# Score matmuls on 128 stacked rows, projections due units ahead, and weight splits moved to ScalarE and GpSimd

## The chip, the cores and the metric

The kernel runs on one core of one Trainium2 chip. The metric is device time in microseconds (us); the time before is 1441.4 us, the median of three runs (1441.32 to 1442.19). Names used below: TensorE is PE, VectorE is DVE, ScalarE is ACT, GpSimd is POOL, SyncE is SP (it issues the DMAs).

## The reference

One layer of a streaming encoder, on 1024 tokens of width 1024, with 16 heads of 64.

```
h = modulate(rms_norm(x), shift, scale);  q,k,v = split(h @ w_in)      # 8 heads A, 8 heads B
A: scores = q k^T / 8 + relative bias, over the own chunk of 64 and the 8 before; softmax; @ v
B: z = q k^T / 8, strictly causal; weights = sigmoid(z_j) * prod_{later keys} sigmoid(-z); @ v
x = x + gate * (concat(rms_norm(A)*g_a, rms_norm(B)*g_b) @ w_out)
h = modulate(rms_norm(x), ...);  g,u = split(causal depthwise conv(h @ w_up))
x = x + gate * ((silu(g) * u) @ w_down);  out = rms_norm(x) * final_g
```

Everything is float32. The kernel works in split numbers: an operand is kept as a high part rounded to the matmul format and a low part, the difference; a product is high x high + high x low + low x high.

## The kernel before, in words

Three stages follow each other. The first loads x, computes the modulation and the norm, transposes h into `hT` (features on partitions) and projects q and k of the first pair of heads. The second is attention, and the only stage whose matmuls the diff changes. The third is the rest of the output projection and the feed-forward part.

In the attention stage there are 8 pairs of heads; pairs 0 to 3 are stick-breaking (B), 4 to 7 chunked (A). Each pair has 16 units: 4 groups `g` of 256 queries, 2 heads `h`, 2 blocks `u` of 128 queries. The loop over `i` (L902) emits for every step the scores of unit i+2, the transposes of unit i's weights (L767) and, after a second block, their product with v (`pv`, L788). Weights of a B unit: sigmoid of z and of -z on ACT, a product scan on DVE (L762), a multiplication on POOL (L765). Weights of an A unit: bias and maximum on DVE, exp on ACT, scaling on POOL (L758).

Between these pieces `fill` (L632) emits matmuls of a list of jobs in a fixed order: projections of q and k (`job_qk`, 48 matmuls of 512 columns for one of them) and of v (`job_v`, 24 matmuls of 256 columns for each block of tokens), then the output projection. A job may not begin before unit `e` and is due at unit `d`; `quota` (L651) spreads the planner's costs (216 and 109 ns a matmul) evenly between these. The order of PE's instructions is the order in which the code emits them; other engines' instructions are placed by a scheduler, in order on each engine's queue. In the background `mods` (L893) accumulates the later modulation on DVE (`macc`, L875) from weights that SP loads one piece ahead.

A weight tile (512 KB) is loaded when a job begins or the one before does (`prefetch`), rounded by DVE (`split_w`, L122) and its low part taken in four pieces (L125), on DVE for q, k and v.

A projected half of 512 tokens lies in PSUM with both heads of the pair on its 128 rows. For the scores a query tile holds q's high part on the 64 rows of the head and its low part on the other 64; the key tile `kh` holds the high part twice. One matmul of 128 rows gives both products with the high keys; a second, of 64 rows, adds high queries x low keys (`kl`):

```
pe(te.matmul, s[:, 0:w], lt, pr.kh[h][:, c], start=True, stop=False)
pe(te.matmul, s[:, 0:w], lt[a], pr.kl[a, c], start=False, stop=True)
```

`evac_q` and `evac_k` (L151, L163) make the high part on ACT and the low part on DVE, and SP's DMAs copy them to the rows where they are wanted: four for a half of q, four for a half of k. The first pair is written in place (L174, L182). There are six query tiles, of which a pair uses four.

Of the kernel before, what the change touches and what calls it, by code (L numbers as in the profile page):

```python
# [12 lines left out]
F32R = mybir.dt.float32r  # L13
# [6 lines left out]
P = 128  # L20
# [6 lines left out]
NP = 8  # L27
# [28 lines left out]
def build(nc, tc, t, ctx):  # L56
# [61 lines left out]
    def split_w(raw, shape, eng=ve):  # L118
# [3 lines left out]
        ve.tensor_copy(wh, raw)  # L122
# [25 lines left out]
    def ex_tile():  # L148
        return mk(pq, [P, HALF + 12], F32R, "ex")[:, 0:HALF]

    def evac_q(ps, hf, qs):  # L151

        x, y = (ex_tile() for _ in range(2))
        sc.activation(x, ps, AF.Copy, scale=HD ** -0.5)
        ve.scalar_tensor_tensor(y, ps, HD ** -0.5, f(x), ALU.mult, ALU.subtract)
        for h in range(2):
            a, b = (lo64, hi64) if h == 0 else (hi64, lo64)
            d = mk(pq, [P, HALF], F32R, "qs")
            sy.dma_start(f(d[a]), f(x[a]))
            sy.dma_start(f(d[b]), f(y[a]))  # L160
            qs[h][hf] = d

    def evac_k(ps, hf, kh, kl):  # L163

        cols = slice(hf * HALF, (hf + 1) * HALF)
        x = ex_tile()
        sc.copy(x, ps)
        ve.tensor_sub(kl[:, cols], ps, f(x))
        for h in range(2):
            a = lo64 if h == 0 else hi64  # L170
            for b in (lo64, hi64):
                sy.dma_start(f(kh[h][b, cols]), f(x[a]))

    def evac_q0(ps, hf, qs):  # L174
        for h in range(2):
            a, b = (lo64, hi64) if h == 0 else (hi64, lo64)
            d = mk(pq, [P, HALF], F32R, "qs")
            sc.activation(d[a], ps[a], AF.Copy, scale=HD ** -0.5)
            ve.scalar_tensor_tensor(d[b], ps[a], HD ** -0.5, f(d[a]), ALU.mult, ALU.subtract)
            qs[h][hf] = d  # L180

    def evac_k0(ps, hf, kh, kl):  # L182
        cols = slice(hf * HALF, (hf + 1) * HALF)
        for h in range(2):
            a, b = (lo64, hi64) if h == 0 else (hi64, lo64)
            sc.copy(kh[h][a, cols], ps[a])
            ve.tensor_sub(kl[a, cols], ps[a], f(kh[h][a, cols]))
            sy.dma_start(f(kh[h][b, cols]), f(kh[h][a, cols]))
# [12 lines left out]
    def new_k(pr):  # L201
        pr.kh = [mk(pq, [P, S], F32R, "kh") for _ in range(2)]
        pr.kl = mk(pq, [P, S], F32R, "kl")
# [243 lines left out]
    for hf in range(2):  # L447
        evac_q0(acc0[0][hf], hf, pairs[0].qs)
        evac_k0(acc0[1][hf], hf, pairs[0].kh, pairs[0].kl)
# [18 lines left out]
    def job_qk(p, which, hfs, w):  # L468
# [3 lines left out]
        for hf in hfs:  # L472
            ps = mk(ps1, [P, HALF], F32, "mm")
            yield from mm3g(ps, [((w[0][0][:, kb], w[0][1][:, kb]), hT[kb][hf]) for kb in range(KB)], 216)
            if which == 0:
                evac_q(ps, hf, pr.qs)
            else:
                evac_k(ps, hf, pr.kh, pr.kl)
# [119 lines left out]
    def add_qk(p):  # L598
        for which in (1, 0):
            add(lambda which=which: pre_qk(p, which), lambda w, which=which: job_qk(p, which, (0, 1), w),  # L600
                48 * 216, 16 * (p - 2) + 14 if which else 16 * (p - 1) + 4, 16 * p - 3)

    def add_v(g):
        got = []

        def pre():
# [4 lines left out]
        for tb in range(TB):  # L611
# [3 lines left out]
    add_v(0)  # L615
    add_qk(1)
    for g in range(1, 4):
        add_qk(2 * g)
        add_v(g)
# [859 lines left out]
```

## Time and profile before

| | |
|---|---|
| median of three runs | 1441.4 us |
| the profiled execution, its own time | 1439.25 us |
| its span (first to last instruction) | 1437.5 us |
| busy: PE, DVE, ACT, POOL | 1362.3, 1231.0, 596.7, 792.9 us |
| attention stage | from about 75 to 648 us |
| granted PE clock over the span | 0.986 |

Busy time is the union of an engine's instructions. Matmuls are pipelined and the end of each is modelled, so PE counts as busy also where one matmul follows the other late; how fast it really goes is read from the distance between starts. An instruction's mean contains the time that it waits inside the engine. "Idle before" is the time in which the engine stood still ahead of an instruction, with what ended it. A tile's name is the program's (`S` scores, `mm` projections, `T` transposes and the product with v, `kt` and `pb` the factors of the weights, `raw`, `wh`, `wl` a weight as loaded, its high and its low part).

### The profile page before, as it was taken

How to read it: one execution, taken by the hardware profiler on the slowest of the kernel's cores; microseconds unless marked ns; L12 is line 12 of the kernel's file. 1: busy time of each engine (PE TensorE's matmuls, PEld its weight loads, DVE VectorE, ACT ScalarE, POOL GpSimd, SP SyncE). 2: the span in 40 equal slices, each digit the busy share in tenths (PEclk: the TensorE clock that was granted, in tenths of full speed). 3: DMA queues.
4: the chain of work that ended last, by engine and by line, in shares of the span. 5: the costliest groups of instructions: out<-in, count | busy, mean ns of one | idle time of the engine just before them, and what ended most of it. 6: DMA issues, size and time to landing. Idle time of an engine off the chain costs nothing.

```text
span 1437.5 us, 19602 instructions
## 1 busy us (share of the span) xinstructions
PE 1362.3 (95%) x6580; PEld 1077.5 (75%) x6580; DVE 1231.0 (86%) x2135; ACT 596.7 (42%) x1246; POOL 792.9 (55%) x678
## 2 busy tenths in 40 slices
PE   5899999999999999999887999999999999999996
PEld 3786788678877887777675777777777777777774
DVE  7879999988878767776789889899998899998888
ACT  5545554555454444342433233333333333233334
POOL 4624343434422225664568666677667677667664
PEclk9999999999999999999989999999999999999998
DMA  8533533343245237646110111111111211111213
GB/s 310 177 118 91 144 89 87 94 123 95 74 126 162 79 112 210 216 155 249 44 45 15 54 50 60 51 45 45 59 52 47 63 45 44 53 56 45 67 37 117
DMA packets 75246, 136.69 MB, mean 95 GB/s; under 512 B 9081, under 2 KB 35849, under 8 KB 75146
## 3 DMA queue, kind: packets, MB, share of 16 engines
q1 hardware_dynamic: 75146, 135.44, 30.6%
q8 instruction: 52, 0.85, 0.2%
q14 instruction: 48, 0.39, 0.1%
HBM read 102.89 MB, written 18.88 MB: 85 GB/s over the span
## 4 chain that ended last, share of the span: by engine, by line
PE 42%; DVE 39%; ACT 6%; issue 5%; DMA 4%; POOL 3%; SPq 0%; DVEq 0%; POOLq 0%; ACTq 0%
PE mm L140 15%; PE up L1086 12%; DVE y L1095 9%; PE T L140 5%; PE dnf L140 5%; PE S L140 4%; DVE x L1220 4%; ACT y L1091 3%; DVE y L1028 3%; DVE ah L1029 2%; DVE kt L762 2%; DVE macc L875 2%; DMA rawm<-ada 2%; DVE ptl L785 1%; DVE wl L125 1%
## 5 line engine op out<-in xcount | busy, mean ns | idle before, releaser
L1220 DVE TENSOR_TENSOR x<-dnf,x 128x512 f32<-128x512 f32 x340 | 222.4, 679 | 0.1
L1095 DVE SCALAR_TENSOR_TENSOR y<-y,sm,y 128x512 f32<-128x512 f32 (+2 forms) x160 | 191.8, 1199 | 28.5 <-ACT y L1091 28.4
L1086 PE MATMUL up<-h,wh 128*128 128x512 f32 x640 | 199.6, 393 | 2.0 <-ACT y L1128 1.2
L1052 POOL TENSOR_TENSOR wl<-raw,wh 128x1024 fp32r<-128x1024 f32 (+1 forms) x62 | 160.1, 2584 | 63.0 <-ACT wh L1050 56.4
L765 POOL TENSOR_TENSOR pb<-pb,kt 128x512 f32<-128x512 f32 (+2 forms) x96 | 91.6, 967 | 158.9 <-DVE kt L762 126.2
L1091 ACT ACTIVATE y<-y,sm 128x512 f32<-128x512 f32 x80 | 65.4, 817 | 262.6 <-DVE y L1167 134.7
L140 PE MATMUL mm<-H,wh 128*128 128x512 f32 x448 | 158.2, 419 | 0.0
L140 PE MATMUL dnf<-dh,ah 128*128 128x512 f32 x336 | 133.6, 397 | 10.5 <-DVE x L1220 9.3
L1086 PEld LDWEIGHTS up<-h,wh 128*128 128x128 f32 x640 | 119.1, 189 | 31.2 <-ACT y L1128 4.2
L140 PE MATMUL dnf<-dl,ah 128*128 128x512 f32 x336 | 134.4, 400 | 2.2 <-POOL dl L1198 0.5
L140 PE MATMUL dnf<-dh,al 128*128 128x512 f32 x336 | 132.7, 395 | 0.9 <-DVE al L1030 0.9
L1086 PE MATMUL up<-h,wl 128*128 128x512 f32 x320 | 125.4, 392 | 0.0
L758 POOL TENSOR_SCALAR pb<-pb,ri 128x640 f32<-128x640 f32 (+2 forms) x64 | 45.6, 713 | 136.0 <-DVE ri L757 84.8
L784 ACT CAST pth<-T 128x512 fp32r<-128x512 f32 (+2 forms) x192 | 86.8, 455 | 65.9 <-PE T L140 64.7
L785 DVE TENSOR_TENSOR ptl<-T,pth 128x512 fp32r<-128x512 f32 (+2 forms) x192 | 98.4, 514 | 10.4 <-ACT pth L784 9.3
L140 PE MATMUL mm<-wh,H 128*128 128x256 f32 x512 | 106.6, 294 | 0.1
L1086 PE MATMUL up<-Tc,wh 128*128 128x512 f32 x320 | 101.0, 397 | 4.6 <-ACT y L1112 4.5
L1198 POOL TENSOR_TENSOR dl<-modt,dh 128x512 fp32r<-128x512 f32 x42 | 65.3, 1554 | 67.9 <-ACT dh L1197 67.9
L1195 POOL TENSOR_TENSOR modt<-modt,modt 128x512 f32<-128x512 f32 x44 | 68.7, 1561 | 58.6 <-DMA modt<-w_down 54.8
L140 PEld LDWEIGHTS mm<-H,wh 128*128 128x128 f32 x448 | 80.1, 189 | 24.0 <-issue 10.8
L140 PE MATMUL T<-ident,pb 128*128 128x128 f32 x528 | 90.4, 275 | 5.8 <-DVE o L810 3.7
L140 PE MATMUL mm<-H,wl 128*128 128x512 f32 x224 | 93.2, 416 | 0.0
(211 smaller groups left out, 3455.5 us busy)
## 6 DMA issues: line engine op xcount, KB each, us to landing
raw<-w_up SPq DMA_DIRECT2D x44, 512.0 KB, 3.6
rawm<-ada SPq DMA_DIRECT2D x128, 128.0 KB, 2.2
modt<-w_down SPq DMA_DIRECT2D x44, 256.0 KB, 2.7
adaw<-ada SPq DMA_DIRECT2D x16, 512.0 KB, 6.6
raw<-w_qk SPq DMA_DIRECT2D x16, 512.0 KB, 3.7
kh<-ex SPq DMA_DIRECT2D x56, 128.0 KB, 2.7
qs<-ex SPq DMA_DIRECT2D x56, 128.0 KB, 2.3
tbd<-wh SPq DMA_DIRECT2D x18, 256.0 KB, 2.3
```

The source lines that it names most:

```text
L140: r = fn(*a, **k)
L758: gp.tensor_scalar(pt[:, 0:n], pt[:, 0:n], ri, 0.0, ALU.mult, ALU.add)
L765: gp.tensor_mul(pt[:, a:b], pt[:, a:b], kt[:, a + 1:b + 1])
L784: sc.copy(dh, tp[:, 0:b - a])
L785: ve.tensor_sub(dl, tp[:, 0:b - a], f(dh))
L1052: late.append(lambda a=a, z=z: ko(gp.tensor_sub(wl[:, a:z], raw[:, a:z], f(wh[:, a:z]))))
L1086: ko(te.matmul(ps, w[x][:, kb], b[kb][y], start=start and n == 0, stop=n == 11, skip_group_check=True))
L1091: ko(sc.activation(y[:, a:z], src[:, a:z], AF.Identity, scale=cw[2][:, b], bias=cb[:, b]))
L1095: ko(ve.scalar_tensor_tensor(y[:, o:z], src[:, o - d:z - d], cw[2 - d][:, b], y[:, o:z], ALU.mult, ALU.add))
L1195: ko(gp.tensor_mul(raw, raw, gbc[hf]))
L1198: ko(gp.tensor_sub(wl, raw, f(wh)))
L1220: r = ve.tensor_add(xc, ps, xc)
```

## The change

Both score matmuls have 128 rows. The key tile holds the high part on the head's rows and the low part on the other 64. There are two query tiles for a half and head: one has high and low parts as the keys have them, the other has them exchanged; the two matmuls add up all four products (low x low is new). `kl` goes. A half of q takes eight DMAs, a half of k four as before; in the first pair the second query tile is made by DMAs and the keys need none. Eight query tiles make one pair, so one set serves all pairs in turn; a half of q is a job of its own, and its evacuation waits until the loop has passed the units that still read the old half. For the last pair the second half goes into a spare value tile. Keys and the first half of q are due five units ahead of the pair; the second half of q three units into it; the jobs of v go half before and half after q. A job without matmuls left is finished at once. Weights of q, k and v, and the first two of the feed-forward stage, are rounded on ACT, and low parts are taken on POOL (one of the first two value weights keeps DVE for its low part).

```diff
-    "qs": 6, "kh": 4, "kl": 2, "ex": 2, "vs": 3, "nm": 3, "rs": 4, "ri": 4,
+    "qs": 8, "kh": 4, "ex": 2, "vs": 3, "nm": 4, "rs": 4, "ri": 4,
...
-    def split_w(raw, shape, eng=ve):
+    def split_w(raw, shape, eng=gp):
...
-        ve.tensor_copy(wh, raw)
+        sc.copy(wh, raw)
...
+    def evac_q(ps, hf, qs, tile_of):
+        x, y = (mk(pq, [P, HALF + 12], F32R, "ex")[:, 0:HALF] for _ in range(2))
         sc.activation(x, ps, AF.Copy, scale=HD ** -0.5)
         ve.scalar_tensor_tensor(y, ps, HD ** -0.5, f(x), ALU.mult, ALU.subtract)
         for h in range(2):
-            a, b = (lo64, hi64) if h == 0 else (hi64, lo64)
-            d = mk(pq, [P, HALF], F32R, "qs")
+            a, b = halves(h)
+            d, e = tile_of(), tile_of()
             sy.dma_start(f(d[a]), f(x[a]))
             sy.dma_start(f(d[b]), f(y[a]))
-            qs[h][hf] = d
+            sy.dma_start(f(e[a]), f(y[a]))
+            sy.dma_start(f(e[b]), f(x[a]))
+            qs[h][hf] = d, e
...
+    def evac_k(ps, hf, kh):
         cols = slice(hf * HALF, (hf + 1) * HALF)
-        x = ex_tile()
+        x, y = (mk(pq, [P, HALF + 12], F32R, "ex")[:, 0:HALF] for _ in range(2))
         sc.copy(x, ps)
-        ve.tensor_sub(kl[:, cols], ps, f(x))
+        ve.tensor_sub(y, ps, f(x))
         for h in range(2):
-            a = lo64 if h == 0 else hi64
-            for b in (lo64, hi64):
-                sy.dma_start(f(kh[h][b, cols]), f(x[a]))
+            a, b = halves(h)
+            sy.dma_start(f(kh[h][a, cols]), f(x[a]))
+            sy.dma_start(f(kh[h][b, cols]), f(y[a]))
...
+            sy.dma_start(f(e[b]), f(d[a]))
+            sy.dma_start(f(e[a]), f(d[b]))
+            qs[h][hf] = d, e
...
-            ve.tensor_sub(kl[a, cols], ps[a], f(kh[h][a, cols]))
-            sy.dma_start(f(kh[h][b, cols]), f(kh[h][a, cols]))
+            ve.tensor_sub(kh[h][b, cols], ps[a], f(kh[h][a, cols]))
...
-            if which == 0:
-                evac_q(ps, hf, pr.qs)
+            if which:
+                evac_k(ps, hf, pr.kh)
+            elif p == NP - 1 and hf == 1:
+                spare = mk(p1, [P, TB, 4, HD], F32R, "vs").rearrange("p (n c) a b -> p n (c a b)", n=4)
+                spare = iter([spare[:, n] for n in range(4)])
+                evac_q(ps, hf, pr.qs, lambda: next(spare))
             else:
-                evac_k(ps, hf, pr.kh, pr.kl)
+                while now[0] < 16 * p - (2 if hf else 10):
+                    yield None
+                evac_q(ps, hf, pr.qs, q_tile)
...
-            add(lambda which=which: pre_qk(p, which), lambda w, which=which: job_qk(p, which, (0, 1), w),
-                48 * 216, 16 * (p - 2) + 14 if which else 16 * (p - 1) + 4, 16 * p - 3)
+        add(lambda: pre_qk(p, 1), lambda w: job_qk(p, 1, (0, 1), w), 48 * 216, 16 * p - 18, 16 * p - 5)
...
+        add(pre, lambda w: job_qk(p, 0, (0,), w), 24 * 216, 16 * p - 10, 16 * p - 5)
+        add(pre, lambda w: job_qk(p, 0, (1,), w), 24 * 216, 16 * p - (10 if last else 4), 16 * p - 3 if last else 16 * p + 3)
...
     for g in range(1, 4):
-        add_qk(2 * g)
-        add_v(g)
-        add_qk(2 * g + 1)
+        got = []
+        add_k(2 * g)
+        add_v(g, range(4), got)
+        add_q(2 * g)
+        add_v(g, range(4, TB), got)
+        add_k(2 * g + 1)
+        add_q(2 * g + 1)
...
-        while ns > 0 and jobs_at[0] < len(jobs):
+        now[0] = i
+        while jobs_at[0] < len(jobs):
             jb = jobs[jobs_at[0]]
+            if ns <= 0 and (jb.it is None or jb.cost > 0):
+                return
...
-            c = next(jb.it, None)
+            c = next(jb.it, 0)
             if c is None:
+                return
+            if c == 0:
                 jobs_at[0] += 1
...
-            lt = pr.qs[h][qb // 4][:, (qb % 4) * P:(qb % 4 + 1) * P]
-            a = lo64 if h == 0 else hi64
-            pe(te.matmul, s[:, 0:w], lt, pr.kh[h][:, c], start=True, stop=False)
-            pe(te.matmul, s[:, 0:w], lt[a], pr.kl[a, c], start=False, stop=True)
+            lt = [x[:, (qb % 4) * P:(qb % 4 + 1) * P] for x in pr.qs[h][qb // 4]]
+            for x in range(2):
+                pe(te.matmul, s[:, 0:w], lt[x], pr.kh[h][:, c], start=x == 0, stop=x == 1)
```

## Rows read from the trace of the kernel before

**Rows 1.** The page, busy time by engine: us, share of span, instructions.

```profile
PE 1362.3 (95%) x6580; PEld 1077.5 (75%) x6580; DVE 1231.0 (86%) x2135; ACT 596.7 (42%) x1246; POOL 792.9 (55%) x678
```

**Rows 2.** Stretches: length; busy PE, PEld, DVE, ACT, POOL; clock, DMA share, GB/s.

```profile
75.00:365.00 290.00, 282.05 (x1597) 222.61 (x1597) 268.78 (x469) 153.71 (x378) 118.51 (x184) 0.99 0.37 104
365.00:648.00 283.00, 279.52 (x1535) 221.94 (x1533) 213.81 (x694) 125.93 (x375) 111.02 (x136) 1.00 0.48 142
```

**Rows 3.** Chain of waits, 75 to 365 us, shares by line.

```profile
by line: PE mm L140 18.0%; DVE kt L762 10.3%; issue 9.7%; DVE macc L875 9.4%; DMA rawm<-ada 9.3%; DVE ptl L785 6.4%; PE T L140 6.3%; DVE wl L125 5.2%; PE S L140 5.0%; DVE wh L122 2.8%; DVE otl L818 2.6%; DVE S L746 2.4%; DVE o L810 2.0%; AC
```

**Rows 4.** PE in order of time, 84 to 92 us: start, length, instruction, operands.

```profile
84.07 0.28 PE L140 MATMUL S<-kh,qs 128*128 128x256 f32 x1
84.28 0.38 PE L140 MATMUL S<-kl,qs 64*128 64x256 f32 x1
84.59 0.39 PE L140 MATMUL mm<-wh,H 128*128 128x256 f32 x1
...
88.03 0.39 PE L140 MATMUL mm<-wh,H 128*128 128x256 f32 x2
...
88.38 0.40 PE L140 MATMUL mm<-wh,H 128*128 128x256 f32 x2
...
90.45 0.44 PE L140 MATMUL S<-kh,qs 128*128 128x512 f32 x1
...
91.24 0.39 PE L140 MATMUL mm<-wh,H 128*128 128x256 f32 x1
```

**Rows 5.** Instructions of tile S: second score matmul, min/median/max ns, shapes.

```profile
L140 PE MATMUL S<-kl,qs x192: 322/439/502, 76.1 to 642.6; 64*128 64x384 f32 x64, 64*128 64x256 f32 x48, 64*128 64x512 f32 x32, 64*128 64x128 f32 x16
```

**Rows 6.** Groups by line, DVE, 75 to 365 us: busy us, mean ns, idle before.

```profile
L125 DVE TENSOR_TENSOR wl<-raw,wh 128x256 fp32r<-128x256 f32 x52 | 26.1, 534 | 0.1
L122 DVE CAST wh<-raw 128x1024 fp32r<-128x1024 f32 x13 | 14.4, 1110 | 0.0
```

**Rows 7.** The same stretch table for L122 (DVE) and L125 (DVE, POOL) alone.

```profile
365.00:648.00 283.00, 5.05 (x7) 1.00 0.48 142
...
365.00:648.00 283.00, 11.15 (x28) 0.00 (x0) 1.00 0.48 142
```

**Rows 8.** Instructions of tiles wh and wl: rounding on ACT, pieces on POOL.

```profile
L1050 ACT CAST wh<-raw x60: 1030/1051/1058, 759.0 to 1386.1; 128x1024 fp32r<-128x1024 f32 x60
...
L125 POOL TENSOR_TENSOR wl<-raw,wh x12: 719/733/1897, 60.6 to 685.6; 128x256 fp32r<-128x256 f32 x12
```

**Rows 9.** POOL and DVE in order of time, 206 to 212 us.

```profile
206.11 2.32 POOL L765 TENSOR_TENSOR pb<-pb,kt 128x512 f32<-128x512 f32 x2 [3.93 <-DVE kt L762]
...
206.26 2.46 DVE L875 SCALAR_TENSOR_TENSOR macc<-rawm,cact,macc 128x256 f32<-128x256 f32 x2
...
211.75 0.47 DVE L875 SCALAR_TENSOR_TENSOR macc<-rawm,cact,macc 128x256 f32<-128x256 f32 x1
```

**Rows 10.** POOL and PE in order of time: one unit of 1024 keys.

```profile
217.78 2.26 POOL L765 TENSOR_TENSOR pb<-pb,kt 128x512 f32<-128x512 f32 x2 [2.23 <-DVE kt L762]
...
221.45 0.60 PE L140 MATMUL T<-ident,pb 128*128 128x128 f32 x4
```

**Rows 11.** Instructions of tile qs: DMA issues on SP's queue, min/median/max ns.

```profile
L160 SPq DMA_DIRECT2D qs<-ex x28: 461/587/602, 130.6 to 560.1; - x28
```

**Rows 12.** DVE and ACT in order of time, 46 to 50 us.

```profile
46.29 1.76 DVE L122 CAST wh<-raw 128x1024 fp32r<-128x1024 f32 x1
...
49.31 0.78 ACT L291 ACTIVATE H<-t,sh_mix,sc_mix 128x512 fp32r<-128x512 f32 x1 [3.28 <-DVE sc_mix L249]
```

**Rows 13.** POOL in order of time, the start of the feed-forward stage.

```profile
678.70 7.66 POOL L125 TENSOR_TENSOR wl<-raw,wh 128x256 fp32r<-128x256 f32 x8 [2.26 <-DVE wh L122]
```

**Rows 14.** Waits, 75 to 365 us: who for whom, total us, times, longest.

```profile
PE T L140 <- DVE ptl L785: 4.1, 6, 1.6
...
DVE macc L875 <- DMA rawm<-ada: 3.9, 5, 1.5
...
PE T L140 <- DVE o L810: 3.7, 5, 1.6
```

More of the change, by code (lines that the diff above doesn't have):

```diff
@@ L146, in build, with halves @@
     lo64, hi64 = slice(0, HD), slice(HD, P)
[L148 to L153, printed above, removed]
+    def halves(h):
+        return (lo64, hi64) if h == 0 else (hi64, lo64)
+    def evac_q(ps, hf, qs, tile_of):
+        x, y = (mk(pq, [P, HALF + 12], F32R, "ex")[:, 0:HALF] for _ in range(2))
         sc.activation(x, ps, AF.Copy, scale=HD ** -0.5)
@@ L202, in new_k @@
         pr.kh = [mk(pq, [P, S], F32R, "kh") for _ in range(2)]
-        pr.kl = mk(pq, [P, S], F32R, "kl")
     cps0, ps0 = pool("ps0", space=PSUM)
@@ L448, in build @@
         evac_q0(acc0[0][hf], hf, pairs[0].qs)
-        evac_k0(acc0[1][hf], hf, pairs[0].kh, pairs[0].kl)
+        evac_k0(acc0[1][hf], hf, pairs[0].kh)
     close(cs)
@@ L596, in add, with add_k, add_q, pre @@
         jobs.append(Job(pre, gen, cost, e, d))
-    def add_qk(p):
-        for which in (1, 0):
-            add(lambda which=which: pre_qk(p, which), lambda w, which=which: job_qk(p, which, (0, 1), w),
-                48 * 216, 16 * (p - 2) + 14 if which else 16 * (p - 1) + 4, 16 * p - 3)
-    def add_v(g):
-        got = []
+    def add_k(p):
+        add(lambda: pre_qk(p, 1), lambda w: job_qk(p, 1, (0, 1), w), 48 * 216, 16 * p - 18, 16 * p - 5)
+    def add_q(p):
+        got = []
+        def pre():
+            if not got:
+                got.append(pre_qk(p, 0))
+            return got[0]
+        last = p == NP - 1
+        add(pre, lambda w: job_qk(p, 0, (0,), w), 24 * 216, 16 * p - 10, 16 * p - 5)
+        add(pre, lambda w: job_qk(p, 0, (1,), w), 24 * 216, 16 * p - (10 if last else 4), 16 * p - 3 if last else 16 * p + 3)
+    def add_v(g, tbs, got):
         def pre():
@@ L609, in pre @@
             return got[0]
-        for tb in range(TB):
+        for tb in tbs:
             add(pre, lambda w, tb=tb: job_v(g, tb, w), 24 * 109, 16 * (2 * g - 1) + 2,
                 32 * g + max(0, 4 * (tb // 2) - 2))
-    add_v(0)
-    add_qk(1)
+    add_v(0, range(TB), [])
+    add_k(1)
+    add_q(1)
     for g in range(1, 4):
-        add_qk(2 * g)
-        add_v(g)
-        add_qk(2 * g + 1)
+        got = []
[5 more added lines that the diff above has]
+        add_q(2 * g + 1)
     add(lambda: None, job_out_b, 192 * 216, 0, 126)
@@ L630, in prefetch @@
                     x.w = jobs[j].w
+    now = [0]
     def fill(i, ns):
-        while ns > 0 and jobs_at[0] < len(jobs):
+        now[0] = i
+        while jobs_at[0] < len(jobs):
             jb = jobs[jobs_at[0]]
+            if ns <= 0 and (jb.it is None or jb.cost > 0):
+                return
             if jb.e > i:
```

12 lines of the change are left out of this document (6 added, 6 removed).

## The prediction

> **What bounds the kernel now.** Four views, from wide to narrow. The page gives TensorE (PE) 95% of the span [rows 1], so I first ask whether PE is also full in the stage that the diff touches. The table by stretches [rows 2] splits the attention stage at the change from stick-breaking pairs (75 to 365 us, 64 units) to chunked pairs (365 to 648 us, 64 units): PE is busy 282.05 of 290 and 279.52 of 283 us at a granted clock of 0.99 and 1.00, VectorE (DVE) 268.78 of 290 in the first half and 213.81 of 283 in the second, ScalarE (ACT) about half, GpSimd (POOL) 40%. So PE sets the pace in both halves, and DVE stands close behind it in the first. The chain of waits [rows 3] says the same of the first half: it hops between PE and DVE (scans, products, weight splits), with no long wait in one place. The stalls of PE that another engine causes are short in sum: the two largest of the first half are 4.1 and 3.7 us [rows 14].
>
> Busy is not the same as well used, so the last view is PE in order of time [rows 4], read by the distance from one start to the next. Projections of 256 columns go at 0.35 us for three (88.03 to 88.38), 0.118 us each. The score pair of 256 columns takes 84.07 to 84.59, 0.52 us, where two such matmuls would take 0.24: 0.28 us lost. The pair of 512 columns takes 90.45 to 91.24, 0.79 us against 4 x 0.118 = 0.47: 0.32 lost. The difference lies round the second matmul, the one on 64 rows: 84.07 to 84.28 is 0.21 (0.09 over) and 84.28 to 84.59 is 0.31 (0.19 over). Every change from 128 to 64 rows and back costs time in which PE counts as busy.
>
> **The change part by part.** All is summed on the profiled execution: span 1437.5 us, its own time 1439.25; the median of the runs shown is 1441.4, 2.15 higher, which I add at the end.
>
> *Stacked scores.* There are 192 pairs, of which 32 have 512 columns [rows 5]. Both matmuls now have 128 rows and as many columns as before, so 160 x 0.28 + 32 x 0.32 = 55 us leave PE. Bounds: 192 x 0.28 = 54 if the wide ones lose no more than the others, 192 x 0.32 = 61 if all lose as much as the widest; below, 192 x 0.19 = 36 if only the return from 64 rows is saved. The trace has no score pair with both on 128 rows; I take 55, because the projections, which change weights at every matmul and accumulate into one tile too, run without a gap.
>
> *Weights.* In the attention stage 52 + 28 low pieces and 13 + 7 roundings leave DVE: 26.1 + 14.4 = 40.5 us in the first half [rows 6], 11.15 + 5.05 = 16.2 in the second [rows 7]. ACT gets 20 roundings of 1.05 us (the same shape, which ACT rounds in the feed-forward stage) = 21 us, POOL 80 pieces of 0.73 = 58.6 us, 38 us of it in the first half [rows 8]. PE does not wait for these, since weights are fetched a job ahead; DVE in the first half falls to 228 us. ACT (153.71 + 14) and POOL (118.51 + 38) stay well under the new span. On ACT a rounding waits for its load as it did on DVE; queued behind it are the sigmoids and the high parts of the transposed weights, for which the unit's scan and PE wait: 0, since a load lands long before its job, at most 20 x 1.05 = 21. What POOL costs DVE is below.
>
> *Does DVE follow?* PE's first half shrinks by 96 pairs, 28 us, to about 262 us. DVE with 228 us is under that, at 87%, if POOL does not slow it. It will a little: two macc updates that lie beside POOL's products take 2.46 us together, one alone takes 0.47 [rows 9], so an overlap can cost up to 0.73 us more, once per piece. Lower bound 0; upper bound 52 x 0.73 = 38 us of DVE, none of it beside anything else. The scan and macc, which read and write SBUF alone, are 19.7 of DVE's 41 points in the chain [rows 3], about half; half of the pieces meeting one of them, for half a piece each, is a quarter of the bound, 10 us, and that I take: DVE 238 of 262, 91%, against 93% now. The stalls should then stay what they are; I add 2 us for units that are shorter by a tenth while the chain scan, product, transpose keeps its length (POOL's products end at 220.04, the transposes start at 221.45, so 1.4 us are in hand [rows 10]).
> The Trainium skill, "SBUF — State Buffer", section "SBUF: two separate sides", says that GpSimd and a VectorE operation with two SBUF inputs take one port pair as an exclusive lock, for the whole instruction. The macc rows agree; by that rule each piece could hold VectorE its full length, and the result is the first rival.
>
> *Queries and keys.* A query half now issues 8 DMAs, not 4; 14 of these halves make 56 more, at 0.59 us each [rows 11] 33 us on SP's queue, beside PE. Keys keep 4. Behind them on SP stand the loads for macc, and behind those DVE: DVE waits 3.9 us for them in the first half now [rows 14]. Bounds: 0, or 14 x 4 x 0.59 = 33 us if each extra issue delays a macc that nobody covers; nearest to the row I take 1 us, included in the 2 us above. Tiles of the queries are now one set: a half's DMA waits until the previous pair has used the same half, but the code emits it only after those scores in PE's order, and 24 matmuls lie between, so 0; the bound above is one unit (4.5 us = 290/64) per pair, 7 x 4.5 = 32.
> In the first pair the keys' DMAs go and the queries' come, before the stage begins; hidden by the 96 value matmuls emitted ahead: 0, at most 4 x 0.59 = 2.4.
>
> *Due times and order.* Total matmul work is the same. Keys are due two units earlier, the second query half six later; over each 32 units the job list holds 4 x 48 x 0.216 + 8 x 24 x 0.109 = 62 us by the planner's own costs, as before, so about 1.95 us per unit either way. The guard before the second query half opens at unit 16p-2; its 24 x 0.216 = 5.2 us at 1.95 per unit last from 16p-4 to that unit, so it hardly holds: 0. If it did hold, PE would lack filler for up to a unit, 0 to 2 us per pair, 14 us. The gain, earlier keys, meets no stall that the waits show: 0 too.
>
> *Outside the stage.* Before it DVE's rounding of the first value weights, 1.76 us, stands ahead of the scale that ACT waits for [rows 12]; on ACT it can sit in that idle time: -1 (bounds -1.8, and +1.1 if ACT puts it ahead of its own work). After it POOL's eight pieces stand ahead of a norm [rows 13]; the pieces were there before, their roundings move: 0 (-2 to +2). The feed-forward stage is untouched.
>
> Sum: -55 + 2 - 1 + 0 = -54: 1439.25 - 54 = 1385.3 for such an execution, 1387 as a median.
>
> **Rivals.**
> 1. *VectorE takes over in the first half, through POOL.* All 52 pieces hold DVE for their whole length: 228 + 38 = 266 us, and the first half stays at 290 x 266/268.8 = 287. It gains 3 instead of 28, the second half 27; with -1 from the start that is -31, 1410 as a median. For it: the macc rows. Against: the pieces are short, and half of DVE's part of the chain is work of another kind.
> 2. *SP's queue.* The 33 us of added issues all reach DVE through macc, and PE behind it: -54 + 33, 1420. Against: such waits sum to 3.9 us in 290 now.
> 3. *Slower: POOL's line.* Place: the products ahead of the transposes stand behind low pieces on the in-order POOL. Price: a piece takes 0.73 to 1.90 us [rows 8]; four at the middle, 1.3, make 5.2 us, less the 1.4 in hand: 3.8 us for each of 20 weight tiles, 76 us: -55 - 1 + 76, 1461 as a median. It decides from 55/20 + 1.4 = 4.2 us per tile, if all four pass ahead of a product. For it: 8 pieces in a row took 7.66 us [rows 13], 3.8 a tile, close to that point. Against: they are separate instructions, so products can pass between them.
> 4. *Stacking saves nothing*: the 0.28 us belongs to the short accumulation over two operands, not to 64 rows. Then 1440. Against it: the projections switch operands at 128 rows without a gap, and the loss is largest after the 64-row one.
>
> **How the numbers follow.** Forecast 0.75 (its own range 1372 to 1398: low if all pairs lose 0.32, -6, and the present 8 us of stalls [rows 14] go, high if the 10 us that POOL costs DVE come to stand on PE's path). Rival 1 0.12, rival 2 0.06, rival 3 0.04, rival 4 0.03. The range 1372 to 1412 leaves out 2, 3, 4 (0.13) and a little on each side of the others, under 0.2. A change under 0.2% (about 3 us) cannot be told from none. Faster is forecast, 1 and 2, 0.93; same is rival 4, 0.03; slower is rival 3, 0.04.
>
> **What would show it.** Right: both score matmuls as 128*128, a 256-column pair in 0.24 us; the two halves near 262 and 256 us with PE still over 95% busy; DVE near 238 us in the first half; weight rows on ACT at 1.05 us and POOL at 0.73. Wrong: macc and scan means up and DVE full (rival 1), macc waiting for its DMA (2), transposes waiting for POOL's products (3), score pairs still at 0.5 us (4).

## The result: 1427.5 us, 0.9% faster, where 1387 was predicted

The changed kernel takes 1427.51 us (median; 1427.01 to 1427.91) against 1441.36 us for the kernel before: ratio 0.9909, 95% interval 0.9893 to 0.9925. It is faster, as forecast, but by 14 us and not by 54, and it lies above the range (1372 to 1412). The profiled execution has a span of 1426.1 us against 1437.5.

### The profile after

The page's line of busy time [rows 1], then the table by stretches [rows 2]; the first of its rows is the start of the stage, the second the 64 stick-breaking units, the third the 64 chunked units.

```profile
PE 1301.0 (91%) x6580; PEld 1070.2 (75%) x6580; DVE 1195.5 (84%) x2031; ACT 617.2 (43%) x1270; POOL 862.0 (60%) x758
```
```profile
75.00:85.00 10.00, 8.22 (x47) 8.26 (x48) 3.92 (x10) 1.48 (x6) 3.16 (x4) 0.62 0.47 158
85.00:353.00 268.00, 243.92 (x1563) 213.00 (x1561) 235.43 (x395) 160.53 (x386) 159.94 (x227) 1.00 0.42 115
353.00:632.00 279.00, 252.96 (x1536) 219.84 (x1535) 205.09 (x647) 131.74 (x379) 128.84 (x165) 0.97 0.55 159
```

PE lost 61 us of busy time, and the stage did not get shorter by that: PE, at 97 and 99% of its stretches before, is now at 91%. VectorE (DVE) is busy for 88% of the first half and 74% of the second.

The score pairs in PE's order of time, the first with 256 columns, the second with 512, each with the projection that follows it [rows 4], and the instructions of tile S [rows 5]:

```profile
87.53 0.40 PE L140 MATMUL S<-kh,qs 128*128 128x256 f32 x2
87.76 0.28 PE L140 MATMUL mm<-wh,H 128*128 128x256 f32 x1
...
97.99 0.68 PE L140 MATMUL S<-kh,qs 128*128 128x512 f32 x2
98.51 0.28 PE L140 MATMUL mm<-wh,H 128*128 128x256 f32 x1
```
```profile
L140 PE MATMUL S<-kh,qs x352: 222/362/882, 85.2 to 593.7; 128*128 128x384 f32 x56, 128*128 128x256 f32 x40, 128*128 128x512 f32 x32, 128*128 128x128 f32 x16
L140 PE MATMUL S<-kh,vs x32: 278/338/422, 596.7 to 631.6; 128*128 128x384 f32 x16, 128*128 128x256 f32 x16
```

All 384 have 128 rows. A pair of 256 columns takes 0.23 us from its start to the next (0.52 before), one of 512 columns 0.52 (0.79 before): 0.29 and 0.27 saved. 160 x 0.29 + 32 x 0.27 = 55 us. Measured on every pair, from its start to the start of the next instruction, the 192 pairs took 129.9 us before; the 190 after the change that have no wait in between take 76.0, which makes 53 us saved. The largest term of the prediction is right.

What came in its place are waits. Summed over every gap of PE above 0.25 us between 64 and 660 us there were 11.9 us before and are 57.9 now. The view of waits, PE's alone, is given for the first half (first fence, [rows 14]) and the second (second fence): who waited for whom, total us, times, longest.

```profile
PE T L140 <- DVE ptl L818: 8.5, 12, 1.2
PE T L140 <- DVE o L843: 8.2, 9, 1.8
PE T L140 <- POOL pb L798: 3.6, 5, 1.3
PE mm L140 <- DVE vs L508: 2.6, 2, 2.1
```
```profile
PE S L140 <- ACT pb L772: 5.6, 6, 2.1
PE T L140 <- DVE ptl L818: 4.5, 5, 2.8
PE mm L140 <- DVE H L518: 4.5, 2, 3.6
PE T L140 <- DVE macc L908: 3.7, 1, 3.7
```

In the first half most of them, 20 of 24 us, are for DVE: the transposes' buffers come free when DVE has taken the low parts (`ptl`) and the outputs (`o`). In the second half they have many owners. The chain of waits of the first half [rows 3] says what DVE itself was held by:

```profile
by line: issue 14.4%; DVE kt L795 13.9%; DMA rawm<-ada 13.1%; PE mm L140 9.6%; DVE macc L908 8.7%; DVE ptl L818 6.7%; POOL pb L798 3.6%; PE T L140 3.3%; ACT kt L780 3.3%; POOL wl L125 2.9%; DVE S L779 2.6%; DVE o L843 2.2%; DVE otl L851 2.0
```

Against [rows 3] PE's projections fell from 18.0% to 9.6%, the scan rose from 10.3% to 13.9% and the loads that macc waits for from 9.3% to 13.1%.

By place, parted at the first score matmul, the 193rd (the first chunked one) and the last, the span's 11.4 us are:

| stretch | before, us | after, us | difference | forecast |
|---|---|---|---|---|
| up to the first score | 75.9 | 85.2 | +9.3 | -1 |
| first half | 285.9 | 267.8 | -18.1 | -28 |
| second half | 281.2 | 279.0 | -2.2 | -27 |
| after the last score | 794.5 | 794.2 | -0.3 | 0 |

The forecast had 2 us more for stalls in the two halves together. The 43 us that are missing from the span lie in all three parts of the stage.

**The start.** PE, ScalarE (ACT), DVE and SP's queue in order of time; the bracket is the wait ahead of the instruction and what ended it.

```profile
76.78 0.55 PE L140 MATMUL mm<-wh,H 128*128 128x256 f32 x1 [7.04 <-DVE vs L508]
...
77.34 0.63 PE L140 MATMUL mm<-wh,H 128*128 128x256 f32 x2
...
77.98 0.63 PE L140 MATMUL mm<-wh,H 128*128 128x256 f32 x2
```
```profile
74.30 1.04 ACT L122 CAST wh<-raw 128x1024 fp32r<-128x1024 f32 x1 [5.39 <-DMA raw<-w_qk]
```
```profile
74.63 0.35 DVE L906 TENSOR_SCALAR macc<-rawm,cact 128x256 f32<-128x256 f32 x1 [4.96 <-DMA rawm<-ada]
```
```profile
69.78 0.55 SPq L188 DMA_DIRECT2D qs<-qs  x1
70.39 0.58 SPq L130 DMA_DIRECT2D raw<-w_qk  x1
71.07 0.86 SPq L898 DMA_DIRECT2D rawm<-ada  x2
```
```profile
72.40:82.60 10.20, 5.82 (x27) 5.86 (x28) 2.99 (x8) 1.91 (x5) 3.16 (x4) 0.50 0.66 221
```

A value block's evacuation (`vs`) needs ACT and then DVE. On both the next instruction in the queue is one that waits for a load, and SP issues these loads behind the eight DMAs of the first queries. PE runs out of buffers and stands for 7.04 us. PE has no more to do here than before: 260 instructions precede the first score in both kernels. Then the granted clock is 0.50, the lower of its two levels, from 72.40 to 82.60 us (the stretch table, the last fence): three projections take 0.64 us there (77.34 to 77.98), and 0.35 at the full clock [rows 4].

**The second half.** One wait there, on PE, DVE and SP's queue:

```profile
442.27 1.19 PE L140 MATMUL T<-macc,ones 128*128 128x256 f32 x2 [3.66 <-DVE macc L908]
```
```profile
438.70 0.15 DVE L790 RECIPROCAL ri<-rs 128x1 f32<-128x1 f32 x1
441.64 0.48 DVE L908 SCALAR_TENSOR_TENSOR macc<-rawm,cact,macc 128x256 f32<-128x256 f32 x1 [2.79 <-DMA rawm<-ada]
```
```profile
432.73 1.02 SPq L898 DMA_DIRECT2D rawm<-ada  x2
...
436.52 0.97 SPq L176 DMA_DIRECT2D kh<-ex  x1
...
438.74 0.43 SPq L898 DMA_DIRECT2D rawm<-ada  x1
```

The load that ends the sum is issued at 438.74, behind the DMAs of a query half and a key half; DVE stands still for it, PE for DVE, and from 441.0 us the granted clock is at the lower level for 6.83 us. In all DVE waited 8.4 us for macc's loads in the first half and 12.6 in the second (3.9 and 1.8 before).

### The profile page after: what moved, and what is told of

It reads as the page before. It is cut to its first block, busy times and chain, and to the rows that moved or that the text cites. A ratio compares the mean times of both kernels' runs of the same rounds, so it can differ in the third digit from the quotient of the medians.

```text
span 1426.1 us, 19745 instructions
## 1 busy us (share of the span) xinstructions
PE 1301.0 (91%) x6580; PEld 1070.2 (75%) x6580; DVE 1195.5 (84%) x2031; ACT 617.2 (43%) x1270; POOL 862.0 (60%) x758
## 4 chain that ended last, share of the span: by engine, by line
DVE 43%; PE 30%; ACT 8%; issue 7%; DMA 7%; POOL 3%; SPq 1%; DVEq 0%; ACTq 0%; POOLq 0%
PE up L1119 13%; DVE y L1128 9%; PE mm L140 7%; PE dnf L140 5%; DMA rawm<-ada 4%; DVE x L1253 4%; ACT y L1124 3%; PE T L140 3%; DVE ah L1062 3%; DVE kt L795 3%; DVE macc L908 2%; DVE y L1061 2%; DVE ptl L818 2%; PE S L140 1%; DVE adaw L251 1%
## 5 line engine op out<-in xcount | busy, mean ns | idle before, releaser
L1128 DVE SCALAR_TENSOR_TENSOR y<-y,sm,y 128x512 f32<-128x512 f32 (+2 forms) x160 | 184.3, 1152 | 24.7 <-ACT y L1124 24.7
L798 POOL TENSOR_TENSOR pb<-pb,kt 128x512 f32<-128x512 f32 (+2 forms) x96 | 94.5, 997 | 97.1 <-DVE kt L795 69.5
L140 PE MATMUL mm<-H,wh 128*128 128x512 f32 x448 | 148.7, 400 | 2.1 <-DVE vs L508 2.1
L140 PE MATMUL mm<-wh,H 128*128 128x256 f32 x512 | 103.5, 292 | 10.5 <-DVE vs L508 9.6
L795 DVE TENSOR_TENSOR_SCAN kt<-kt 128x128 f32<-128x128 f32 (+3 forms) x64 | 96.4, 1506 | 9.8 <-ACT kt L780 7.4
L140 PE MATMUL S<-kh,qs 128*128 128x384 f32 (+5 forms) x352 | 99.6, 364 | 4.8 <-ACT pb L772 4.8
```

Of the source, the lines that this page charges most:

```text
L140: r = fn(*a, **k)
L795: ve.tensor_tensor_scan(r, r, r, 1.0, ALU.mult, ALU.bypass)
L798: gp.tensor_mul(pt[:, a:b], pt[:, a:b], kt[:, a + 1:b + 1])
L1128: ko(ve.scalar_tensor_tensor(y[:, o:z], src[:, o - d:z - d], cw[2 - d][:, b], y[:, o:z], ALU.mult, ALU.add))
```

## The experiments

Times are ratios to the kernel before on the same chip, with the 95% interval; edits are on the changed kernel unless it says otherwise, and `...` marks lines left out of one. The expectations speak of these theories. A: the weights' move costs what stacking gains. B: the chain of one unit (scores, scan, product, transposes) is the limit, whatever engine is free. C: the gain is lost at places, the stage's start and the queue of SP. D: DVE bounds the first half, in work and in waits at the head of its queue.

### The two parts of the change apart

k1_split_dve, stacking alone (with its new due times and DMAs):

```diff
-    def split_w(raw, shape, eng=gp):
+    def split_w(raw, shape, eng=ve):
...
-        sc.copy(wh, raw)
+        ve.tensor_copy(wh, raw)
```

> The changed kernel (1427.5 us) with the weights of q, k and v rounded and their low parts taken on VectorE again; stacked scores and new due times stay. Theory A (the move of the weights ate the gain: at the start of the attention stage ScalarE stands on a rounding that waits 5.4 us for its load, so that the first scores start at 85.2 instead of 75.9 us, and later GpSimd's pieces delay the chain): the first scores near 76 us and some 25 us of TensorE's waits gone as well, 1393 us. Theory B (the units' own chain is the limit once the scores are short, whoever splits weights): only the start comes back, 1418 us; up to 1425 if VectorE's 57 us more come onto the chain.

Measured: 0.9959 (0.9943 to 0.9974). k2_only_weights, the kernel before with these two lines of the change and nothing else:

> The kernel before (1441.4 us) with the move of the weights alone: rounding on ScalarE, low parts on GpSimd. Theory A: the start loses 9 us as in the changed kernel and the chain some more: 1450 to 1465 us. Theory B: 1450 us at most, and 1441 if the relief of VectorE (57 us) gives back what the start costs. If neither the start nor the chain suffers: 1440.

Measured: 0.9969 (0.9954 to 0.9984). Each part alone is worth 0.3 to 0.4%, both 0.9%. A falls: moving the weights is a gain. In k2 the first half shrinks by 5.4 us though PE's matmuls are those of before, and the first score stays at 75.8 us; in k1 it shrinks by 5.8, and PE waits there 11.9 us for `o` and 10.4 for `ptl`. So in the first half DVE limits stacking, and limited the kernel before too. The second half of k1 is 279.0 us, as in the changed kernel: there, too, it is not the weights' move that takes the gain of stacking.

Half of the weights' move each. k3_round_dve has the roundings on DVE, k4_low_dve the low pieces:

```diff
-        sc.copy(wh, raw)
+        ve.tensor_copy(wh, raw)        # k3
...
-    def split_w(raw, shape, eng=gp):
+    def split_w(raw, shape, eng=ve):   # k4
```

> The changed kernel with the rounding of the weights back on VectorE, low parts still on GpSimd. Theory A: the wait for the load leaves ScalarE, the first scores start near 76 us, GpSimd's pieces stay: 1418 us. Theory B: the same 1418 us, since only the start comes back. Both fall if the start stays at 85 us.

> The changed kernel with rounding on ScalarE as it has it, but low parts on VectorE again. Theory A (with GpSimd's pieces as the cause of the later waits): the start still loses 9 us, some 25 us of the later waits go, 1402 us. Theory B: start and later waits stay, 1427 to 1432 us.

Measured: k3 0.9993 (0.9982 to 1.0003), k4 0.9918 (0.9898 to 0.9939). With k1 and the changed kernel these make a square. Moving the rounding to ACT gains with the low pieces on either engine: 0.9959 to 0.9918 with them on DVE, 0.9993 to 0.9909 with them on GpSimd (POOL). Moving the pieces gains nothing that can be told from none (0.9918 to 0.9909), and loses while the rounding is on DVE (0.9959 to 0.9993). So it is the rounding that must leave DVE. The first halves of k3 and k4 hold about as much DVE work, 246.9 and 245.2 us, and are 276.3 and 269.6 us long. What makes this difference is not shown: DVE waits there 10.9 us for macc's loads in k3 and 5.3 in k4, and a rounding itself waits for its load only once, at the start.

### More and less work for DVE

k6_in_place adds work to ACT and DVE and takes DMAs from SP's queue, by writing every pair as the first one is written:

```diff
-                evac_k(ps, hf, pr.kh)
+                evac_k0(ps, hf, pr.kh)
...
-                evac_q(ps, hf, pr.qs, q_tile)
+                evac_q0(ps, hf, pr.qs, q_tile)
```

> The changed kernel with every pair's queries and keys evacuated straight to the rows where they are wanted, as the first pair's are: a half of q takes 4 DMAs instead of 8, a half of k none instead of 4, at the price of one more instruction of 64 rows on ScalarE (0.58 us) and on VectorE (0.68 us) for each of 28 halves. Theory C (SP's queue delays the loads of the background accumulation and of the output weights in the second half: TensorE waits 3.7 us at 442 us and 5.9 us at 544 to 552 us, and goes at half clock for 13.6 us behind them): these waits go, 1411 to 1415 us. Theory D (VectorE is the bound): its 19 us more cost up to 10, 1430 to 1437 us.

Measured: 0.9996 (0.9985 to 1.0007). Fewer DMAs do not pay for the work: the first half is 278.8 us, 11 longer than in the changed kernel, with 11.0 us more of DVE. The second half, with 8.9 us of waits for macc's loads in place of 12.6, stays at 279.0.

k8_no_macc leaves out all of macc's multiply-adds but the first of each eight; its loads stay. The later modulation vectors are so left out of the output.

```diff
                 if kb == 0:
                     ve.tensor_scalar(acc, w, cact[:, 0:1], None, ALU.mult)
-                else:
-                    ve.scalar_tensor_tensor(acc, w, cact[:, kb:kb + 1], acc, ALU.mult, ALU.add)
```

> The changed kernel without the multiply-adds of the background accumulation (all but the first piece of each eight are left out, the loads stay): some 60 us less on VectorE, 80 of 112 instructions in the first half, and no waits for those loads. Theory D (VectorE bounds the first half): its waits there (24 us) shrink to what they were before the change (8 us), 1404 us or lower. Theory C alone (places): only the wait at 442 us goes, 1420 us.

Measured: 0.9641 (0.9625 to 0.9658). The same edit on the kernel before is k14_before_no_macc:

> The kernel before without macc's multiply-adds (its loads stay; the vectors that they sum are left out of the output). If TensorE held both halves before, as the prediction said: the time falls by no more than the stalls there, 8 us, to 1432 or above, against the 40 us that the same edit took from the changed kernel. If VectorE already held the first half before: 15 us or more, 1425 or below, with the first half well under 286 us.

Measured: 0.9895 (0.9876 to 0.9913), 14.4 us, at the edge of the outcome that speaks for DVE. Stretch tables of k14 (first fence) and k8 (second), first and second half:

```profile
76.00:349.00 273.00, 273.00 (x1558) 216.89 (x1559) 225.08 (x395) 154.29 (x374) 114.93 (x184) 1.00 0.39 108
349.00:629.00 280.00, 278.09 (x1535) 221.25 (x1534) 197.76 (x644) 125.73 (x373) 104.39 (x134) 1.00 0.48 142
```
```profile
83.00:328.00 245.00, 239.37 (x1561) 215.09 (x1561) 197.63 (x333) 162.69 (x389) 162.27 (x228) 0.99 0.47 127
328.00:591.00 263.00, 249.27 (x1533) 218.24 (x1533) 184.57 (x603) 130.46 (x377) 127.65 (x164) 0.97 0.58 169
```

Read as a square: with macc the change is worth 0.9%, without it 0.9641 / 0.9895 = 0.9743, 2.6%. The first half of k14 has PE busy for 273.00 of 273: that is PE's own length or more, and the kernel before was 12 us over it. From there to k8 the first half shrinks by 28 us, which is the forecast for stacking. B falls as the limit of the first half: the chain of a unit has the same instructions in k8, and the units are shorter. In the second half the gain is 16 of 27 us even so (279.4 to 263.1).

k10_pace runs macc in five units of eight in place of four of five, so that a fifth of it moves from the first half to the second:

```diff
-PACE = 4, 5
+PACE = 5, 8
```

> The changed kernel with the background accumulation spread thinner, a step in 5 of 8 units instead of 4 of 5, so that about a fifth of it (11 us of VectorE) moves from the first half of the attention stage to the second. Theory D (without that accumulation the stage was 40 us shorter because VectorE bounds the first half): the first half 8 us shorter, the second at most a few longer, 1421 us. If the waits for its loads are what counts: no change, 1427.

Measured: 0.9860 (0.9841 to 0.9880), better than the change. First half 262.3 us against 267.8, PE's idle time there 19.4 against 24.1.

k11_mask_pe moves the causal mask's addition from DVE to a third matmul of the last score block (identity x mask) on PE:

```diff
...
+            if masked:
+                pe(te.matmul, s[:, w - P:w], identr, smaskr, start=False, stop=True)
...
-                if part == parts - 1:
-                    ve.tensor_add(s[:, w - P:w], s[:, w - P:w], smask)
```

> The changed kernel with the causal mask of the stick-breaking scores added by TensorE (a third matmul of 128 columns into the same bank, 0.06 us) instead of by VectorE (64 times 0.29 us): 18.5 us less on VectorE in the first half, 4 more on TensorE, and one step less between the scores and the sigmoids. Theory D: the first half 10 to 13 us shorter, 1415 to 1418 us. If waits for loads are what counts: 1427 to 1431 us.

Measured: 0.9939 (0.9921 to 0.9958), no gain and perhaps a loss. The first half kept its length (268.5 us). DVE's work there fell by 11 us, but it waited 17.7 us for macc's loads instead of 8.4; PE's waits fell by 6 us, but its own work grew by 6, with one matmul more for each masked unit.

Taken together, these runs show how far DVE's work sets the first half of a kernel with stacked scores (us in that half):

| run | DVE busy | length |
|---|---|---|
| k8 | 197.3 | 244.9 |
| k15 (below) | 219.5 | 257.5 |
| k10 | 227.6 | 262.3 |
| the change | 235.4 | 267.8 |
| k4 | 245.2 | 269.6 |
| k6 | 246.4 | 278.8 |
| k3 | 246.9 | 276.3 |
| k1 | 258.0 | 280.1 |

From k8 to k1 the half grows by 0.58 us for each us of DVE. All runs with stacked scores lie within 6 us of that line but k11, whose PE has more to do, 8 above it.

### Waits for loads

k7_deep_loads issues macc's loads three ahead in four buffers, in place of one ahead in two:

```diff
-    ... "rawm": 2, ...
+    ... "rawm": 4, ...
...
-            w = load(0)
+            ahead = [load(kb) for kb in range(3)]
...
-                nw = load(kb + 1) if kb + 1 < KB else None
+                w = ahead.pop(0)
+                if kb + 3 < KB:
+                    ahead.append(load(kb + 3))
...
-                w = nw
```

> The changed kernel with the loads of the background accumulation issued three pieces ahead instead of one (four buffers). Theory C: the accumulation no longer waits behind the queries' and keys' DMAs, TensorE's wait of 3.7 us at 442 us and the half clock behind it go: 1420 us, or lower if other waits of VectorE come from there. Theory D: 1427 us, no change.

Measured: 0.9895 (0.9877 to 0.9914). Against the change's 0.9909 the intervals overlap; the second half fell from 279.0 to 272.0 us, with 4.3 us of waits for macc's loads in place of 12.6. The first rose to 272.7, though the same waits fell from 8.4 to 3.3; the granted clock was at the lower level there for 17.1 us (0 in the changed kernel), which costs up to 8.5.

k12_wout_early issues the first two loads of the output weights ahead of the last query half's DMAs:

```diff
...
-            wo[fb, 0] = load_wout(fb, 0)
+            wo[fb, 0] = load_wout(fb, 0, raws.pop(0) if raws else None)
...
-    add(lambda: None, job_out_b, 192 * 216, 0, 126)
+    add(lambda: [load_w(t["w_out"][kb, :, 0:HALF], [P, HALF]) for kb in (4, 5)], job_out_b, 192 * 216, 0, 126)
```

> The changed kernel with the first two loads of the output weights issued before the last pair's query DMAs instead of behind them on SP's queue. Theory C: TensorE's waits at 544 to 552 us (5.9 us) and the half clock behind them (6.8 us) shrink, 1420 to 1423 us. If the attention outputs, which the same matmuls need, are as late: 1427 us.

Measured: 0.9915 (0.9895 to 0.9935), no gain. PE's wait for these weights fell from 4.5 to 3.1 us only, and the second half was 280.9 us.

k16_pace_deep is k10 and k7 together. k15_both has the deep loads, macc in two units of three from unit 8 on (as many steps as in k10), and the late first weights of k9 below:

```diff
-        if i >= 0 and i % PACE[1] < PACE[0]:
+        if i >= 8 and i % PACE[1] < PACE[0]:   # PACE = 2, 3
```

> The changed kernel with macc in five units of eight and its loads three ahead: 1416 to 1418 if the two single gains (7 and 3.5 us) add; 1420 if the deeper loads only help what the slower pace already covers. The start as in the changed kernel, first score at 83 to 85 us.

> The changed kernel with all three: loads of macc three ahead in four buffers, macc from unit 8 in two units of three, first key weights fetched late. If the waits are in VectorE's queue (its work and its waits for loads): the gains of the single edits add to some part, 1412 to 1418, first half near 262 us, second near 270. If they overlap: 1420, as with the slower pace alone.

Measured: k16 0.9821 (0.9803 to 0.9840), k15 0.9823 (0.9798 to 0.9849); medians 1414.2 and 1414.1 us, with k18 below the best of those that compute the whole output. Relative to the change k10 gains 0.5%, k7 0.1%, both 0.9%. Whether they do more together than apart is within the noise.

k10 and k16 also part the two things that macc costs. In the first half k16 has no wait for macc's loads left (7.2 us in k10) and is no shorter, 263.2 against 262.3 us; 17.1 us at the lower clock, against 6.8, cost it up to 5. In the second half these waits fall from 12.3 to 4.0 us, and the half from 277.0 to 270.7, much as from the change to k7. So in the first half it is chiefly macc's work on DVE that counts, in the second the waits for its loads.

### The start of the stage

k5_vs_first raises the first value evacuations in the scheduler's order, k9_late_prefetch fetches the first key weights only once the units run:

```diff
+            with tc.high_priority(offset=400 if g == 0 else 0):   # k5, around the two lines of vs
...
-                for j in range(jobs_at[0] + 1, len(jobs)):
+                for j in range(jobs_at[0] + 1, len(jobs) if i > -3 else 0):   # k9
```

> The changed kernel (1427.5 us) with the evacuations of the first value projections put ahead of the weight rounding on ScalarE and of the accumulations on VectorE. Theory C (the gain was lost at places: first the start of the attention stage, where an evacuation of v stands behind an instruction that waits for a load, TensorE waits 7.0 us and then goes at half clock for 10.2 us): the first scores start near 76 instead of 85 us and the time falls by 9 us to 1418. Theory D (VectorE bounds the first half, so that a lead of TensorE at the start is given back there): 1424 to 1428 us.

> The changed kernel (1427.5 us) with the first weights of keys loaded and rounded only after the first four value blocks have been emitted, so that their rounding can't stand ahead of the evacuations of v. Theory C (the start is a place of its own): first scores near 76 instead of 85 us, 1418 us. Theory D (VectorE bounds the first half and gives the lead back): 1424 to 1427 us.

Measured: k5 0.9928 (0.9909 to 0.9946), k9 0.9928 (0.9904 to 0.9953): neither is told from the change. In both the order on ACT did not change, so they tell nothing of the cause; in k9 the rounding still waits 5.31 us for its load ahead of `vs`, the first score comes at 84.0 us, and PE waits 6.3 us for `vs`.

k13_start is k9 with macc from unit 8 on (`i >= 8`, PACE 4, 5):

> The changed kernel, with the weights of the first key job fetched only once the units are under way and macc's first load and update moved from unit 0 to unit 8: at the stage's start neither ScalarE nor VectorE then has an instruction that waits for a load ahead of a value evacuation. If those two waits (5.4 and 5.0 us) make the 7.0 us wait of TensorE and the later first score: first score near 76 to 78 us instead of 85.2, no half clock there, about 7 us less, near 1420. If the start is late because the queries are now stacked later: first score stays at 83 to 85 and the time stays within 3 us of 1427.

Measured: 0.9868 (0.9845 to 0.9890), but hardly by the start: the first score came at 82.9 us, where runs that did not touch the start have it at 83.4 (k1) to 85.4 (k10). The rounding still stood ahead of the evacuation (ACT in order of time):

```profile
73.91 1.04 ACT L122 CAST wh<-raw 128x1024 fp32r<-128x1024 f32 x1 [5.24 <-DMA raw<-w_qk]
```

k17_early_load loads these weights 15 us earlier, ahead of the query DMAs:

```diff
     split_v0(1)
+    raw1 = [load_w(t["w_qk"][1, 1], [P, KB, P])]
...
-        return [split_w(load_w(t["w_qk"][p, which], [P, KB, P]), [P, KB, P])]
+        raw = raw1.pop() if raw1 else load_w(t["w_qk"][p, which], [P, KB, P])
+        return [split_w(raw, [P, KB, P])]
```

> The changed kernel, with the first key weights loaded right after the first value weights, some 20 us earlier, ahead of the first pair's query DMAs on SP's queue; nothing else differs. If ScalarE's rounding, which waited 5.4 us for that load ahead of a value evacuation, makes the start late: first score near 76 to 78 us instead of 85.2, no half clock there, 7 us less or so: 1419 to 1421. If stacking the queries itself makes the start late, or macc's load still does: first score at 83 or later, 1425 to 1428.

Measured: 0.9920 (0.9898 to 0.9942), no gain; first score at 83.8 us. ACT's rounding no longer waits, and DVE's macc does, ahead of the evacuation (DVE in order of time):

```profile
72.58 0.35 DVE L908 TENSOR_SCALAR macc<-rawm,cact 128x256 f32<-128x256 f32 x1 [3.42 <-DMA rawm<-ada]
73.90 0.49 DVE L910 SCALAR_TENSOR_TENSOR macc<-rawm,cact,macc 128x256 f32<-128x256 f32 x1 [0.96 <-DMA rawm<-ada]
74.42 0.29 DVE L509 TENSOR_TENSOR vs<-mm,vs 128x128 fp32r<-128x128 f32 x1
```

k18_all has the early load and k15's macc:

> The same early load, with macc in two units of three from unit 8 and its loads three ahead in four buffers. If the start, the pace and the deep loads are separate losses: 1405 to 1408 (1414 for the last two, less 7). If they are one: 1412 to 1414.

Measured: 0.9823 (0.9801 to 0.9845), 1412.9 us, as k15 and k16; first score at 83.3 us. Again macc stands ahead of the evacuation (DVE in order of time):

```profile
77.19 0.35 DVE L910 TENSOR_SCALAR macc<-rawm,cact 128x256 f32<-128x256 f32 x1 [6.84 <-DMA rawm<-ada]
77.46 0.28 DVE L509 TENSOR_TENSOR vs<-mm,vs 128x128 fp32r<-128x128 f32 x1
```

So the traces name the start's cause, an instruction that waits for a load ahead of `vs` on one of two in-order queues, and each of these edits left or put another such instruction there. In k2, with scores and DMAs of before, the first score is at 75.8; ACT rounds the next weights there too, but behind the first evacuations and scores, and without a wait (ACT in order of time):

```profile
77.78 1.05 ACT L122 CAST wh<-raw 128x1024 fp32r<-128x1024 f32 x1
```

No run with stacked queries had that order, so that it would give back the 9 us stays unproved.

## Why the prediction was wrong

- **The terms of work were right.** Stacking freed 53 to 55 us of PE, as forecast. DVE's first half was forecast at 238 us and is 235.4, with 74 macc instructions in it where there were 80 (6 x 0.69 = 4). Roundings took 1.05 us on ACT and pieces 0.74 on POOL, in these groups of tiles wh and wl [rows 8]:

```profile
L122 ACT CAST wh<-raw x24: 1031/1051/1086, 46.2 to 671.8; 128x1024 fp32r<-128x1024 f32 x24
...
L125 POOL TENSOR_TENSOR wl<-raw,wh x92: 717/737/1664, 61.2 to 675.0; 128x256 fp32r<-128x256 f32 x92
```

- **The step that failed** is "The stalls should then stay what they are; I add 2 us", with "So PE sets the pace in both halves" before it. PE's stalls rose by 46 us (11.9 to 57.9), 7 of them at the start, and that is the miss. I compared DVE's sum with the shortened half, 238 of 262, and called 91% enough because 93% had been. But the kernel before was not free of DVE at 93%: k14 shows that macc cost 12 us of its first half. My reading, which fits k14 and k8 but which no run shows by itself, is that PE's excess work had covered DVE's uneven moments, a scan of 2.3 us, an evacuation or a macc update that waits, and that stacking took just this cover. The "1.4 us in hand" [rows 10] were read from one unit.
- **How much macc accounts for.** By the medians the forecast missed by 40 us (54 against 14). Without macc the change gains 2.6% instead of 0.9%: 24 of the 40. The first half then shrinks by all that was forecast. What is left is mostly the start (75.8 in k14, 82.8 in k8, forecast -1: 8 us) and the second half (16 of 27: 11 us).
- **The second half** had DVE at 74% and still returned 2 of 27 us. PE's idle time there rose from 3.5 to 26.0 us, and round the long waits the clock was low for 17.1 us (0 before), which costs at most half of that, 8.5. I had not looked for a cover that goes there at all: 213.81 of 283 us [rows 2] seemed safe. Leaving macc out gives 16 us back. Part of that are the waits for its loads, which rose by 10.8 us: with them down to 4.3 and 4.0 us (k7, k16) the half is 6 to 7 us shorter. The rest (ACT's exp, the output weights, transposes) was seen but not taken apart; it stays open.
- **The start** was forecast at -1 and cost +9.3. I priced the first pair's query DMAs at "0, at most 4 x 0.59" as time on SP's queue; their price was what stood behind them, loads for which ACT and DVE waited ahead of PE's evacuations. For the rounding that had moved to ACT I named the waiting of sigmoids and took 0; the value evacuation, on the same queue, I did not list.
- **Rivals.** 1, DVE takes over in the first half, came nearest, though by macc and not by POOL's pieces: without macc the first half gains all that was forecast (k8), and with the pieces back on DVE the time is the same (k4). The sharing exists. DVE's groups by shape in the first half (busy us, mean ns), of the change (first fence) and of k4 (second) [rows 6, 9]:

```profile
L908 DVE SCALAR_TENSOR_TENSOR macc<-rawm,cact,macc 128x256 f32<-128x256 f32 x65 | 45.1, 694 | 9.4 <-DMA rawm<-ada 8.4
...
L795 DVE TENSOR_TENSOR_SCAN kt<-kt 128x512 f32<-128x512 f32 x8 | 12.2, 1527 | 3.8 <-ACT kt L780 3.8
...
L795 DVE TENSOR_TENSOR_SCAN kt<-kt 128x384 f32<-128x384 f32 x8 | 10.1, 1263 | 2.2 <-ACT kt L780 2.2
```
```profile
L908 DVE SCALAR_TENSOR_TENSOR macc<-rawm,cact,macc 128x256 f32<-128x256 f32 x65 | 41.7, 641 | 6.0 <-DMA rawm<-ada 5.3
...
L795 DVE TENSOR_TENSOR_SCAN kt<-kt 128x512 f32<-128x512 f32 x8 | 10.2, 1274 | 0.1
...
L795 DVE TENSOR_TENSOR_SCAN kt<-kt 128x384 f32<-128x384 f32 x8 | 7.6, 952 | 1.7 <-ACT kt L780 1.7
```

  Over all of DVE's instructions in that half but the pieces, durations add up to 255.5 us in the change and 245.2 in k4: 10.3 us, where the term was taken as 10 and bounded at 38. By the lock that the Trainium skill, "SBUF — State Buffer", section "SBUF: two separate sides", describes, every piece that meets such an operation could hold it up for its whole length, an estimate of 33 us for the 44 pieces in that half; the traces show a third of it. Rival 2, SP's queue: DVE's waits for macc's loads went from 5.7 to 21.0 us over both halves, half of its 33. That the added DMAs make them is not shown: in the first half they are 7.3 us in k2, with the DMAs of before, and in the second 8.9 in k6, with fewer DMAs than before. Rival 3 (transposes behind POOL's products) is 3.6 us of waits in the first half, rival 4 nothing.

## What to carry to other kernels

An engine that counts as 95% busy because its instructions follow each other badly is hiding the unevenness of the engines next to it: before pricing a saving there, take the neighbour's load away in thought (or in a run) and ask how long each engine's own length is, then expect the sum to stop well above the longer of them when the two lie within a tenth (here PE needs 245 us or less, by k8, DVE is busy for 235, and the half takes 268). For every instruction moved to an in-order queue list what it waits for and what stands behind it, at the stage's start above all, where loads are freshest. When two engines are close, spreading the second one's background work (here one number, macc's pace, and deeper loads: 1414 us) is worth as much as the change itself.

## What was not expected of the hardware

- During a long wait of PE the granted clock goes to the lower level (1.2 GHz) and stays there when work has resumed: 10.24 us with the wait of 7.04 at the start, 6.83 with that of 3.66 (442.27), 6.83 with that of 3.57 (551.42). Before the change the stage had 3.4 us of it in all. At the start 5.8 us of it lie after 76.78; by 0.35 us in place of 0.64 for the same three matmuls they cost 2.6 us on top of the wait.
- Scans slowed beside POOL's pieces more than macc did: against k4 those of 512 columns by 20% (1274 to 1527 ns), of 384 by 33% (952 to 1263), macc by 8% (641 to 694), while scans of 1024 columns did not slow (2343 and 2317).
